# Attention on one Trainium2 core: four score banks, two product banks, and row sums from a column of ones beside the values

## The chip, the cores and the metric

The kernel runs on one core of a Trainium2 chip. The metric is the device time of one execution in microseconds; the median of repeated runs counts. The core has TensorE (PE, with PEld for its weight loads), VectorE (DVE), ScalarE (ACT), GpSimd (POOL) and SyncE (SP), each with a queue of its own that it works through in order. TensorE writes its results to PSUM, which this program divides into eight banks of 128 partitions by 512 numbers of 4 bytes.

## The reference

One step of a streaming encoder: attention, an MLP, a gated linear recurrence, and a second MLP, each with a norm before it and a sum with its input behind it. There are 1024 prompt frames and 64 frames of a running stream, 1088 in all, 1024 features, 16 query heads in 4 groups that share a key and value head of 64. Only the attention bears on the change. A chunk is 64 frames; a frame reads its own chunk and the two before it, so 192 keys. Every head has a learned sink, which enters the denominator and no value.

```python
def banded_sink_attention(q, k, v, valid, sinks):
    B, N, Q = q.shape[:3]
    qg = q.reshape(B, N, Q, N_KV, GROUP, HEAD_DIM)
    s = jnp.einsum('bnqkgd,bnskd->bnkgqs', qg, k,
                   preferred_element_type=jnp.float32) * (HEAD_DIM ** -0.5)
    s = jnp.where(valid[None, :, None, None, None, :], s, -jnp.inf)
    sink = sinks.astype(jnp.float32).reshape(N_KV, GROUP)[None, None, :, :, None, None]
    m = jnp.maximum(jnp.max(s, axis=-1, keepdims=True), sink)
    e = jnp.exp(s - m)
    p = e / (jnp.sum(e, axis=-1, keepdims=True) + jnp.exp(sink - m))
    o = jnp.einsum('bnkgqs,bnskd->bnqkgd', p.astype(v.dtype), v)
    return o.reshape(B, N, Q, N_HEADS, HEAD_DIM)
```

## The kernel before

The program runs attention (to about 356 us of the profile), the first MLP, the recurrence and the second MLP, one after the other. All products with weight matrices are done in two parts: a weight and an input are each split into a rounded half and a rest (`whi`, `wlo`, `xh`, `xl`), and each 128 x 128 block takes three matmuls (lines 93 to 95) into one bank of the pool `mm` (lines 107 and 108). VectorE takes a finished bank away. The pool `mm` has three banks for the whole program. The attention's own pool `psA` has five: two `sc`, two `pt`, one `po`. An MLP adds five banks to `mm`, the recurrence four of its own.

**Attention.** `heads(g)` goes over group g in nine steps m. Steps 0 to 7 take two chunks each (index i), step 8 the running stream. The four heads of a group stand as two tiles u = 0 and 1: the queries and keys of tile u lie in partitions 64u to 64u + 63, each tile with two heads of 64 frames, so 128 rows of scores. `scores(m)` does, for a step:

- the scores (line 306): for each i and u a matmul over 64 partitions into the bank `sc` of tile u, 192 columns (64 and 128 in step 0);
- the row maximum (311, 313), its comparison with the sink (316), and the sink's exponent (317) on VectorE;
- the exponentials on ScalarE (321), one for each i and u, from `sc` into `p`; each also sums its row into `den` (`accum_out`), which the profile shows as a second instruction, ACTIVATION_READ_ACCUMULATOR;
- the sink's exponential (324), its sum with `den` (325) and the reciprocal (326).

`values_(m)` does the rest: for each u it transposes `p` in three blocks into a bank `pt` (334), which ScalarE copies to `ptts` (335); it multiplies these with the values, `vone` and `vtok`, into `po` (340); VectorE multiplies `po` with `den` into `ob` (353); `ob` is transposed into a bank `pq` (358, the same bank as `po`), and ScalarE copies that into `pair` (363), the group's output. `vone` is built by GpSimd in each step (line 290): it holds the middle 64 keys of the two chunks, apart, so that one matmul serves both.

**What sets the order.** The step's scores are written one step ahead of its values. `mixed()` interleaves `heads(g)` with a generator of other products: the queries of group g + 1 for g = 0 to 2 (`q_group`), the output product `mix_out` for g = 3. That is only the order of writing. The framework then goes over the program with a scheduler of its own, which puts each engine's instructions in the order in which it takes them to become ready; a tile of a pool is ready when a buffer is free. So the number of buffers of a pool bears on the order of every engine. In what follows, fill means products that stand between the steps of `heads`. Behind the last step of group 3, `mix_out` takes its fourth input (`take`, which calls `split`, 162 and 163) and adds the products with `wb` (408), six matmuls each.

Of the kernel before, what the change touches and what calls it, by code (L numbers as in the profile page):

```python
# [8 lines left out]
F32 = mybir.dt.float32  # L9
# [4 lines left out]
ALU = mybir.AluOpType  # L14
AX = mybir.AxisListType
PSUM = bass.MemoryType.PSUM

P = 128
# [9 lines left out]
NKV = 4  # L28
# [7 lines left out]
class Trunk:  # L36
    def __init__(self, ctx, tc, A, O):
        self.ctx, self.tc, self.nc, self.A, self.O = ctx, tc, tc.nc, A, O
        nc = self.nc
        self.cp = ctx.enter_context(tc.tile_pool(name="const", bufs=1))  # L40
        self.wp = ctx.enter_context(tc.tile_pool(name="weights", bufs=2))
        cp = self.cp
        nc.scalar.preload_act_table_set("natural_log_exp_and_others")
        self.mm = ctx.enter_context(tc.tile_pool(name="mm", bufs=3, space=PSUM))
        self.more, self.turn = None, 0

        self.queue = nc.sync
# [51 lines left out]
    def scaled(self, c):  # L99
        if c in self.due:  # L100
            self.due.remove(c)
            self.norm_scale(c)
# [49 lines left out]
    def norm_scale(self, c):  # L152
        nc = self.nc
        s, n = self.CH[c]
        ps = self.bank()
        nc.tensor.matmul(ps[:, :n], self.ones[:], self.ss[:, s:s + n], start=True, stop=True)  # L156
        self.inv_root(self.rstd[:, s:s + n], ps[:, :n], n, D)
# [8 lines left out]
    def attention(self):  # L166
        nc, tc, A, O = self.nc, self.tc, self.A, self.O
        with ExitStack() as ctx:
# [50 lines left out]
            vone = [ap.tile([P, 2, 64], F32, name=f"vone{i}") for i in range(3)]  # L219
# [3 lines left out]
            def values(t):  # L223
                nc.sync.dma_start(O["v"][t], vt[:, t, TP - 128:T])
                for b in range(0, 9, 4):
                    pt = psA.tile([P, 4, P], F32, name="pt", tag="pt", bufs=2)
                    if b < 8:
                        for i in range(4):
                            nc.tensor.transpose(pt[:, i, :], vt[:, t, (b + i) * P:(b + i + 1) * P], self.ident[:])
                        nc.scalar.copy(vtok[:, b:b + 4, t * P:(t + 1) * P], pt[:])  # L230
                    else:
                        nc.tensor.transpose(pt[:, 0, :], vt[:, t, T - P:T], self.ident[:])
                        nc.scalar.copy(vtok[64:, 9, t * P:(t + 1) * P], pt[64:, 0, :])
# [48 lines left out]
            def heads(g, qs):  # L282
                o = self.xp[g] = self.pair(g)

                def scores(m):
                    cs = (2 * m, 2 * m + 1) if m < 8 else (16,)
                    ni = len(cs)
                    if m < 8:
                        vo, dv = vone[m % 3], slice(g * 64, g * 64 + 64)
                        nc.gpsimd.tensor_copy(vo[:64, 0, :], vtok[:64, m, dv])  # L290
                        if m:
                            nc.gpsimd.tensor_copy(vo[64:, 1, :], vtok[64:, m - 1, dv])
# [26 lines left out]
                    for u in range(2):  # L319
                        for i, (kn, off) in enumerate(sp):  # L320
                            nc.scalar.activation(pb[:, u, off:off + kn], ps[u][:, i, :kn], AF.Exp,  # L321
                                                 bias=nmax[:, u, i:i + 1], scale=0.125,
                                                 accum_out=den[:, u, i:i + 1])
                    nc.scalar.activation(es[:, :, :ni], es[:, :, :ni], AF.Exp)
                    nc.vector.tensor_add(den[:, :, :ni], den[:, :, :ni], es[:, :, :ni])
                    nc.vector.reciprocal(den[:, :, :ni], den[:, :, :ni])
                    return m, cs, ni, 2 * ni, den, pb

                def values_(m, cs, ni, nu, den, pb):
                    kts = range(0 if 0 < m < 8 else 1, 3)  # L330
                    for u in range(2):
                        pt = psA.tile([P, 4, P], F32, name="pt", tag="pt", bufs=2)
# [4 lines left out]
                    dv = slice(g * 64, g * 64 + 64)  # L337
                    for u in range(2):
# [3 lines left out]
                        if m == 0:  # L342
                            term(1, po[:, 0, u, :64], vone[0][:, 0, :], True, True)
                            term(2, po[:, 1, u, :64], vtok[:, 0, dv], True, True)
                        elif m < 8:
                            term(1, po[:, :, u, :64], vone[m % 3][:], True, False)
                            term(0, po[:, 0, u, :64], vtok[:, m - 1, dv], False, False)
                            term(2, po[:, 1, u, :64], vtok[:, m, dv], False, True)
                        else:
                            term(1, po[:, 0, u, :64], vtok[:, 9, dv], True, False)  # L350
                            term(2, po[:, 0, u, :64], vtok[:, 8, dv], False, True)
                    ob = ap.tile([P, 4, 64], F32, name="ob", tag="ob")
                    nc.vector.tensor_tensor(ob[:, :nu, :].rearrange("p (i u) d -> p i u d", u=2), po[:, :ni, :, :64],
                                            den[:, :, :ni].rearrange("p u i -> p i u").unsqueeze(3)
                                            .to_broadcast([P, ni, 2, 64]), ALU.mult)
# [559 lines left out]
```

## Time and profile before

| | us |
|---|---|
| runs without a profile, three | 2586.03, 2586.2, 2589.6 (median 2586.2) |
| profiled execution, its time | 2588.19 |
| profiled execution, its span | 2586.4 |
| mean clock granted to TensorE | 0.997 of full |
| attention, from the first instruction to the end of its fill | 0 to about 350 |

In the rows of the profile, a group reads: line, engine, operation, output<-inputs, shape, x count, then busy time in us and the mean of one in ns, then idle time of the engine just before and what ended it. A row of the timeline reads: start in us, duration in us, engine, line, operation, output<-inputs, shape, x count, and in brackets the idle time before it and the releaser. Several records of one kind in a row are joined, and the duration of a matmul goes to its modelled end, so that neighbours overlap; the distance between two starts is what an instruction cost the queue. A matmul of two fp32 operands leaves two records. In a row like "ACT p L321: 5.1, 16" under a line stand the idle us before a line's instructions, by what ended them, and how often.

### The profile page before, as it was taken

The page shows a single profiled execution, that of the slowest core. Times are in us where ns is not written, and L with a number is a line of the kernel's source. Part 1 is how long each engine was busy: PE and PEld are TensorE (multiplying, and loading weights), DVE is VectorE, ACT ScalarE, POOL GpSimd, SP SyncE. Part 2 cuts the span into 40 slices and gives each one's busy share as a digit, 9 for nine tenths or more (in the row PEclk, how much of TensorE's full clock was granted, in tenths as well). Part 3 has the DMA queues.
Part 4 walks back from the last instruction along what each step waited for, and adds up shares of the span by engine and source line. Part 5 has one row for each costly group of instructions (what it writes and reads, how often), then busy time and mean ns, then how long its engine had stood idle before and what let it go on. Part 6 is the DMA issues. An engine that isn't in the chain of part 4 may idle for free.

```text
span 2586.4 us, 40870 instructions
## 1 busy us (share of the span) xinstructions
PE 2555.1 (99%) x16788; PEld 2495.6 (96%) x16788; DVE 1324.6 (51%) x2693; ACT 913.8 (35%) x2071; POOL 61.6 (2%) x152
## 2 busy tenths in 40 slices
PE   8999999999999999999999999999999999999998
PEld 7998899999999999999999999998999999999997
DVE  7555455333333333376677777876433333333337
ACT  5336544122122122154555555635312211211223
POOL 3201100000000000000000000000000000000000
PEclk9999999999999999999999999999999999999999
DMA  5312111111111111131111111121111111111112
GB/s 167 85 46 65 37 63 41 42 49 41 49 41 46 45 41 50 42 109 49 36 36 37 37 37 37 41 93 34 50 41 50 41 45 46 41 50 41 50 41 82
DMA packets 84074, 134.07 MB, mean 52 GB/s; under 512 B 25440, under 2 KB 36320, under 8 KB 82208
## 3 DMA queue, kind: packets, MB, share of 16 engines
q1 hardware_dynamic: 79456, 119.17, 14.6%
q0 software_dynamic: 4432, 12.29, 1.6%
q8 instruction: 132, 2.16, 0.4%
q14 instruction: 54, 0.44, 0.1%
HBM read 114.39 MB, written 10.49 MB: 48 GB/s over the span
## 4 chain that ended last, share of the span: by engine, by line
PE 85%; DVE 1%; ACT 0%; issue 0%; ACTq 0%; DVEq 0%
PE mm L93 26%; PE mm L94 26%; PE mm L95 26%; PE pb L587 2%; PE pb L551 1%; PE pb L674 1%; PE pb L646 1%; PE pb L676 1%; PE pb L689 0%; PE pb L618 0%; DVE y L733 0%; PE pv L529 0%; PE pb L633 0%; PE mm L156 0%; PE pb L560 0%
## 5 line engine op out<-in xcount | busy, mean ns | idle before, releaser
L93 PE MATMUL mm<-xh,whi 128*128 128x362 f32 (+3 forms) x2944 | 978.7, 333 | 13.7 <-ACT whi L83 12.1
L94 PE MATMUL mm<-xl,whi 128*128 128x362 f32 (+3 forms) x2944 | 973.0, 331 | 0.0
L95 PE MATMUL mm<-xh,wlo 128*128 128x362 f32 (+3 forms) x2944 | 970.3, 330 | 0.0
L93 PEld LDWEIGHTS mm<-xh,whi 128*128 128x128 f32 x2944 | 554.0, 188 | 22.1 <-ACT whi L83 12.1
L94 PEld LDWEIGHTS mm<-xl,whi 128*128 128x128 f32 x2944 | 554.1, 188 | 5.5 <-issue 3.3
L95 PEld LDWEIGHTS mm<-xh,wlo 128*128 128x128 f32 x2944 | 554.5, 188 | 3.2 <-issue 0.9
L83 ACT CAST whi<-raw 128x512 fp32r<-128x512 f32 (+1 forms) x374 | 211.5, 611 | 812.2 <-PE mm L94 804.3
L93 PE MATMUL mm<-hh,whi 128*128 128x362 f32 (+1 forms) x1440 | 472.8, 328 | 0.0
L94 PE MATMUL mm<-hl,whi 128*128 128x362 f32 (+1 forms) x1440 | 472.6, 328 | 0.0
L95 PE MATMUL mm<-hh,wlo 128*128 128x362 f32 (+1 forms) x1440 | 470.6, 327 | 0.0
L727 DVE TENSOR_TENSOR pair<-pair,mm 128x362 f32<-128x362 f32 (+3 forms) x384 | 204.1, 532 | 423.4 <-PE mm L95 423.1
L95 PEld LDWEIGHTS mm<-hh,wlo 128*128 128x128 f32 x1440 | 271.4, 188 | 0.0
L93 PEld LDWEIGHTS mm<-hh,whi 128*128 128x128 f32 x1440 | 270.5, 188 | 0.0
L94 PEld LDWEIGHTS mm<-hl,whi 128*128 128x128 f32 x1440 | 270.1, 188 | 0.0
L718 DVE SCALAR_TENSOR_TENSOR r<-mm,ss 128x362 f32<-128x362 f32 (+1 forms) x192 | 102.5, 535 | 319.0 <-PE mm L95 319.0
L84 DVE TENSOR_TENSOR wlo<-raw,whi 128x512 fp32r<-128x512 f32 (+1 forms) x374 | 240.2, 678 | 4.3 <-ACT whi L83 3.6
L719 ACT ACTIVATE r<-r 128x362 f32<-128x362 f32 (+1 forms) x192 | 96.8, 505 | 353.7 <-DVE r L718 353.7
L721 DVE TENSOR_TENSOR hl<-r,hh 128x362 fp32r<-128x362 f32 (+1 forms) x192 | 102.6, 535 | 142.4 <-ACT hh L720 142.4
L720 ACT CAST hh<-r 128x362 fp32r<-128x362 f32 (+1 forms) x192 | 94.9, 495 | 5.8
L492 DVE TENSOR_TENSOR z<-mm,ss 128x384 f32<-128x384 f32 (+1 forms) x96 | 50.7, 532 | 67.1 <-PE mm L95 66.3
L408 DVE TENSOR_TENSOR pair<-pair,mm 128x384 f32<-128x384 f32 (+1 forms) x84 | 43.8, 529 | 39.1 <-PE mm L95 38.7
L321 ACT ACTIVATE p<-sc,nmax 128x192 f32<-128x192 f32 (+2 forms) x136 | 54.4, 414 | 22.9 <-DVE nmax L316 20.0
(215 smaller groups left out, 2114.4 us busy)
## 6 DMA issues: line engine op xcount, KB each, us to landing
raw<-in_w_up SPq DMA_DIRECT2D x128, 256.0 KB, 3.0
raw<-in_w_down SPq DMA_DIRECT2D x128, 256.0 KB, 2.8
raw<-in_w_in SPq DMA_DIRECT2D x64, 256.0 KB, 2.7
raw<-in_w_qkv POOLq DMA_DIRECT2D x24, 256.0 KB, 3.3
pair<-in_x SPq DMA_DIRECT2D x4, 1088.0 KB, 5.2
x_keep<-pair SPq DMA_DIRECT2D x4, 1088.0 KB, 4.7
pair<-x_keep SPq DMA_DIRECT2D x4, 1088.0 KB, 6.9
out_y<-y SPq DMA_DIRECT2D x16, 208.0 KB, 1.9
```

The lines of the kernel that those rows point to most:

```text
L83: nc.scalar.copy(hi[:, a:a + b, :], raw[:, :b, :])
L84: nc.vector.tensor_sub(lo[:, a:a + b, :], raw[:, :b, :], hi[:, a:a + b, :].bitcast(F32))
L93: nc.tensor.matmul(ps[:, :n], wh, ih[:, s:s + n], start=i == 0, stop=False)
L94: nc.tensor.matmul(ps[:, :n], wh, il[:, s:s + n], start=False, stop=False)
L95: nc.tensor.matmul(ps[:, :n], wl, ih[:, s:s + n], start=False, stop=i == last)
L321: nc.scalar.activation(pb[:, u, off:off + kn], ps[u][:, i, :kn], AF.Exp, bias=nmax[:, u, i:i + 1], scale=0.125, accum_out=den[:, u, i:i + 1])
L587: nc.tensor.matmul(psa[r:r + 64 - hh, i // 2, :].rearrange("p (s t) -> p s t", t=hh), d[:, i * 64:i * 64 + 64 - hh], dv[:, i * ns:(i + 1) ...
L718: nc.vector.scalar_tensor_tensor(y, ps, 0.0, self.rstd[:, s:s + n], ALU.max, ALU.mult)
L719: nc.scalar.activation(y, y, AF.Square)
L720: nc.scalar.copy(hh[:, s:s + n], y)
L721: nc.vector.tensor_sub(hl[:, s:s + n], y, hh[:, s:s + n].bitcast(F32))
L727: nc.vector.tensor_add(self.x(d)[:, s:s + n], self.x(d)[:, s:s + n], ps)
```

## The change

The banks are dealt out anew. `mm` keeps two banks instead of three; a new `add_banks` gives the MLPs six further ones instead of five and the recurrence one, so that these have eight, and seven with the recurrence's four, as they had. In attention there are four banks `sc`, one `pt`, one `po`. The first products and norms use `sc` and `pt`.

The row sum no longer comes from the exponentials. The values get a 65th column of ones (`vtok` and `vone` are 65 wide), so that `po` has the row sum in its column 64. The sum with the sink's exponential and the reciprocal move from `scores` to `values_`, behind `po` and before `ob`; they run once for a step as before.

```diff
-        self.mm = ctx.enter_context(tc.tile_pool(name="mm", bufs=3, space=PSUM))
-        self.more, self.turn = None, 0
+        self.mm = ctx.enter_context(tc.tile_pool(name="mm", bufs=2, space=PSUM))
+        self.more, self.turn, self.extra = None, 0, 0
...
+    def add_banks(self, ctx, name, n):
+        self.more, self.turn, self.extra = ctx.enter_context(self.tc.tile_pool(name=name, bufs=n, space=PSUM)), -1, n
+        ctx.callback(setattr, self, "extra", 0)
 
 
     def bank(self):
-        self.turn = (self.turn + 1) % 8
-        pool = self.more if self.more and self.turn < 5 else self.mm
+        self.turn = (self.turn + 1) % (2 + self.extra)
+        pool = self.more if self.turn < self.extra else self.mm
         return pool.tile([P, 512], F32, name="mm", tag="mm")
...
-                    b = psA.tile([P, 512], F32, name="v", tag=("sc", "pt")[c - 1], bufs=2) if c else None
+                    b = psA.tile([P, 512], F32, name="v", tag="sc", bufs=4) if c else None
...
-                self.scaled(c)
+                self.scaled(c, psA.tile([P, 512], F32, name="n", tag="pt", bufs=1))
...
-            vtok = ap.tile([P, 10, 256], F32, name="vtok")
-            nc.vector.memset(vtok[0:64, 9, :], 0.0)
-            nc.sync.dma_start(vtok[:, 8, :], A["cache_v"])
+            vtok = ap.tile([P, 10, NKV, 65], F32, name="vtok")
+            nc.vector.memset(vtok[:, :, :, 64:], 1.0)
+            nc.vector.memset(vtok[0:64, 9, :, :], 0.0)
+            nc.sync.dma_start(vtok[:, 8, :, :64], A["cache_v"].rearrange("p (g d) -> p g d", d=64))
...
-            vone = [ap.tile([P, 2, 64], F32, name=f"vone{i}") for i in range(3)]
+            vone = [ap.tile([P, 2, 65], F32, name=f"vone{i}") for i in range(3)]
...
-                    den = ap.tile([P, 2, 2], F32, name="den", tag="den", bufs=3)
                     es = ap.tile([P, 2, 2], F32, name="es", tag="es", bufs=3)
-                    ps = [psA.tile([P, 2, 256], F32, name="sc", tag="sc", bufs=2) for u in range(2)]
+                    ps = [psA.tile([P, 2, 256], F32, name="sc", tag="sc", bufs=4) for u in range(2)]
...
                             nc.scalar.activation(pb[:, u, off:off + kn], ps[u][:, i, :kn], AF.Exp,
-                                                 bias=nmax[:, u, i:i + 1], scale=0.125,
-                                                 accum_out=den[:, u, i:i + 1])
+                                                 bias=nmax[:, u, i:i + 1], scale=0.125)
                     nc.scalar.activation(es[:, :, :ni], es[:, :, :ni], AF.Exp)
-                    nc.vector.tensor_add(den[:, :, :ni], den[:, :, :ni], es[:, :, :ni])
-                    nc.vector.reciprocal(den[:, :, :ni], den[:, :, :ni])
-                    return m, cs, ni, 2 * ni, den, pb
-
-                def values_(m, cs, ni, nu, den, pb):
+                    return m, cs, ni, 2 * ni, es, pb
+
+                def values_(m, cs, ni, nu, es, pb):
...
-                            term(1, po[:, :, u, :64], vone[m % 3][:], True, False)
-                            term(0, po[:, 0, u, :64], vtok[:, m - 1, dv], False, False)
-                            term(2, po[:, 1, u, :64], vtok[:, m, dv], False, True)
+                            term(1, po[:, :, u, :65], vone[m % 3][:], True, False)
+                            term(0, po[:, 0, u, :65], vtok[:, m - 1, g, :], False, False)
+                            term(2, po[:, 1, u, :65], vtok[:, m, g, :], False, True)
...
+                    den = ap.tile([P, 2, 2], F32, name="den", tag="den", bufs=2)
+                    dn = den[:, :ni, :]
+                    nc.vector.tensor_tensor(dn.unsqueeze(3), po[:, :ni, :, 64:65],
+                                            es[:, :, :ni].rearrange("p u i -> p i u").unsqueeze(3), ALU.add)
+                    nc.vector.reciprocal(dn, dn)
                     ob = ap.tile([P, 4, 64], F32, name="ob", tag="ob")
                     nc.vector.tensor_tensor(ob[:, :nu, :].rearrange("p (i u) d -> p i u d", u=2), po[:, :ni, :, :64],
-                                            den[:, :, :ni].rearrange("p u i -> p i u").unsqueeze(3)
-                                            .to_broadcast([P, ni, 2, 64]), ALU.mult)
+                                            dn.unsqueeze(3).to_broadcast([P, ni, 2, 64]), ALU.mult)
...
+            self.add_banks(ctx, "mmB", 1)
...
-            self.more, self.turn = ctx.enter_context(tc.tile_pool(name=f"mm{layer}", bufs=5, space=PSUM)), -1
-            ctx.callback(setattr, self, "more", None)
+            self.add_banks(ctx, f"mm{layer}", 6)
```

**What moves in the queues.** The rows are instructions in program order on one engine: line, operation, output<-inputs, shape, x count; numbers behind a name tell tiles apart. Line numbers behind the changed part are 1 to 5 higher after.

PE before, group 1 around the scores of step 4 (tiles sc_1859 and sc_1860, which stand side by side within products of the next group):

```order
L334 MATMUL pt_1791<-ident_81,p0_456 128x128 x2
L358 MATMUL pq_1668<-ident_81,ob_1666 128x128 x2
L334 MATMUL pt_1791<-ident_81,p0_456 128x128
L334 MATMUL pt_1796<-ident_81,p0_456 128x128 x3
L306 MATMUL sc_1859<-kd1_467,qs_1069 128x192 x2
L306 MATMUL sc_1860<-kd1_467,qs_1069 128x192 x2
L93 MATMUL mm_2647<-xh5_70,whi_2332 128x384
```

PE after, the second score tile of the same step (sc_1857; the first, sc_1856, stands 35 rows earlier, with products and transposes between):

```order
L94 MATMUL mm_2743<-xl3_76,whi_2317 128x320
L335 MATMUL pt_1740<-ident_81,p1_458 128x128 x3
L340 MATMUL po_1656<-vone0_459,ptts_456 128x65
L340 MATMUL po_1656<-vtok_452,ptts_456 128x65
L340 MATMUL po_1656<-vone0_459,ptts_456 128x65
L340 MATMUL po_1656<-vtok_452,ptts_456 128x65
L310 MATMUL sc_1857<-kd1_468,qs_1064 128x192 x2
L95 MATMUL mm_2743<-xh3_68,wlo_2318 128x320
```

The two score tiles of a step have moved apart, and the scores run further ahead of the values. Of the 28 steps with two chunks and 192 keys, 13 have their score tiles as neighbours before and two after; the scores stand in 54 blocks before and 72 after.

PE before, a step without fill (group 1, scores of step 7, sc_2065 and sc_2066):

```order
L334 MATMUL pt_1997<-ident_81,p1_457 128x128 x3
L358 MATMUL pq_1895<-ident_81,ob_1893 128x128 x2
L334 MATMUL pt_2002<-ident_81,p1_457 128x128 x3
L306 MATMUL sc_2065<-kd1_467,qs_1069 128x192 x2
L306 MATMUL sc_2066<-kd1_467,qs_1069 128x192 x2
L340 MATMUL po_1961<-vone1_459,ptts_455 128x2x64
```

PE after, the same scores (sc_2062 and sc_2063):

```order
L310 MATMUL sc_2062<-kd1_468,qs_1064 128x192 x2
L335 MATMUL pt_1876<-ident_81,p1_458 128x128 x3
L363 MATMUL pq_1808<-ident_81,ob_1806 128x128 x2
L335 MATMUL pt_1946<-ident_81,p0_457 128x128 x3
L310 MATMUL sc_2063<-kd1_468,qs_1064 128x192 x2
L340 MATMUL po_1881<-vone0_459,ptts_456 128x2x65
```

Between the transposes of one step's second tile and the next step's first there stands pq alone, and both go through the one bank `pt`; steps 7 and 8 of group 1 and steps 0 to 7 of group 2 look like this after.

PE before, behind the last fill product of attention (group 3, steps 7 and 8):

```order
L358 MATMUL pq_3488<-ident_81,ob_3486 128x128 x2
L340 MATMUL po_3551<-vtok_452,ptts_455 128x64 x4
L358 MATMUL pq_3558<-ident_81,ob_3556 128x128
L93 MATMUL mm_3762<-xh6_71,whi_3736 128x320
L93 MATMUL mm_3770<-xh6_71,whi_3736 128x384
```

PE after, the same place:

```order
L335 MATMUL pt_3469<-ident_81,p1_458 128x128 x3
L363 MATMUL pq_3426<-ident_81,ob_3424 128x128 x2
L335 MATMUL pt_3541<-ident_81,p0_457 128x128 x2
L340 MATMUL po_3474<-vone1_460,ptts_456 128x2x65
L340 MATMUL po_3474<-vtok_452,ptts_456 128x65 x2
...
L335 MATMUL pt_3545<-ident_81,p0_457 128x128 x2
L363 MATMUL pq_3486<-ident_81,ob_3484 128x128 x2
L340 MATMUL po_3549<-vtok_452,ptts_456 128x65 x4
L363 MATMUL pq_3559<-ident_81,ob_3557 128x128
L93 MATMUL mm_3763<-xh6_71,whi_3737 128x320
```

The transposes of steps 7 (second tile) and 8 and the values of step 7 now follow the last fill product. Outside attention a few rows of PE change places at the starts of stages.

More of the change, by code (lines that the diff above doesn't have):

```diff
@@ L150, in inv_root, with norm_scale @@
         nc.vector.tensor_mul(out, out, y[:, :n])
-    def norm_scale(self, c):
+    def norm_scale(self, c, ps=None):
         nc = self.nc
         s, n = self.CH[c]
-        ps = self.bank()
+        ps = ps or self.bank()
         nc.tensor.matmul(ps[:, :n], self.ones[:], self.ss[:, s:s + n], start=True, stop=True)
@@ L225, in values @@
                 for b in range(0, 9, 4):
-                    pt = psA.tile([P, 4, P], F32, name="pt", tag="pt", bufs=2)
+                    pt = psA.tile([P, 4, P], F32, name="pt", tag="pt", bufs=1)
                     if b < 8:
@@ L229, in values @@
                             nc.tensor.transpose(pt[:, i, :], vt[:, t, (b + i) * P:(b + i + 1) * P], self.ident[:])
-                        nc.scalar.copy(vtok[:, b:b + 4, t * P:(t + 1) * P], pt[:])
+                        nc.scalar.copy(vtok[:, b:b + 4, 2 * t:2 * t + 2, :64], pt[:].rearrange("p b (h d) -> p b h d", d=64))
                     else:
                         nc.tensor.transpose(pt[:, 0, :], vt[:, t, T - P:T], self.ident[:])
-                        nc.scalar.copy(vtok[64:, 9, t * P:(t + 1) * P], pt[64:, 0, :])
+                        nc.scalar.copy(vtok[64:, 9, 2 * t:2 * t + 2, :64], pt[64:, 0, :].rearrange("p (h d) -> p h d", d=64))
             kd = [ap.tile([P, 1216], F32, name=f"kd{g}") for g in range(NKV)]
@@ L288, in scores @@
                     if m < 8:
[L289 to L290 removed]
+                        vo = vone[m % 3]
+                        nc.gpsimd.tensor_copy(vo[:64, 0, :], vtok[:64, m, g, :])
                         if m:
[L292 removed]
+                            nc.gpsimd.tensor_copy(vo[64:, 1, :], vtok[64:, m - 1, g, :])
                     nmax = ap.tile([P, 2, 2], F32, name="nmax", tag="nmax", bufs=3)
[L295 removed]
                     es = ap.tile([P, 2, 2], F32, name="es", tag="es", bufs=3)
[L297 removed]
+                    ps = [psA.tile([P, 2, 256], F32, name="sc", tag="sc", bufs=4) for u in range(2)]
                     sp = []
@@ L336, in values_ @@
                     po = psA.tile([P, 2, 2, 128], F32, name="po", tag="po")
-                    dv = slice(g * 64, g * 64 + 64)
                     for u in range(2):
```

14 lines of the change are left out of this document (7 added, 7 removed).

## The prediction

> **What bounds the kernel now.** I read the page first: the busy shares, then the chain that ended last.
>
> ```profile
> PE 2555.1 (99%) x16788; PEld 2495.6 (96%) x16788; DVE 1324.6 (51%) x2693; ACT 913.8 (35%) x2071; POOL 61.6 (2%) x152
> PE 85%; DVE 1%; ACT 0%; issue 0%; ACTq 0%; DVEq 0%
> ```
>
> TensorE is the bound, and ScalarE and VectorE stand in the chain with 1% between them. An edit therefore counts by what it does to TensorE's queue. Only attention changes in substance (the other stages keep eight or seven banks as before), so the second view is the busy time by stretch of attention, columns as in the header.
>
> ```profile
> core 0: us, PE busy (x) PEld busy (x) DVE busy (x) ACT busy (x) POOL busy (x), PEclk, DMA share, GB/s
> 90.00:216.00 126.00, 126.00 (x825) 115.81 (x824) 67.87 (x188) 53.78 (x210) 15.56 (x40) 1.00 0.22 57
> 216.00:245.00 29.00, 27.71 (x180) 23.27 (x178) 13.16 (x48) 19.64 (x85) 2.34 (x10) 0.94 0.31 78
> 262.00:292.00 30.00, 29.21 (x204) 25.46 (x203) 15.44 (x54) 18.71 (x80) 1.99 (x8) 1.00 0.11 38
> 330.00:356.00 26.00, 24.14 (x165) 23.46 (x164) 9.59 (x21) 9.27 (x27) 1.61 (x3) 1.00 0.09 31
> ```
>
> While a group of heads has products of the next group to fill with (90 to 216), PE is busy for all of 126 us. In the two stretches without fill it idles 1.3 and 0.8 us, and 1.9 us at the tail. So there are two regimes: with fill, only PE's own instruction time counts; without it, the round trips through ScalarE and VectorE count too. The third view is the timeline of PE around the score products (L306).
>
> ```profile
> 98.79 0.93 PE L306 MATMUL sc<-kd,qs 64*128 64x192 f32 x8
> 99.64 0.55 PE L334 MATMUL pt<-ident,p 128*128 128x128 f32 x3
> 123.40 0.91 PE L306 MATMUL sc<-kd,qs 64*128 64x192 f32 x4
> 124.24 0.42 PE L93 MATMUL mm<-xh,whi 128*128 128x320 f32 x1
> 124.49 0.31 PE L94 MATMUL mm<-xl,whi 128*128 128x320 f32 x1
> 124.64 0.31 PE L95 MATMUL mm<-xh,wlo 128*128 128x320 f32 x1
> 124.88 0.91 PE L306 MATMUL sc<-kd,qs 64*128 64x192 f32 x4
> 125.73 0.42 PE L93 MATMUL mm<-xh,whi 128*128 128x320 f32 x1
> ```
>
> This is the row on which most of the forecast rests. A step m has two score tiles; tile u uses rows 64u to 64u+63 of the array. (Each fp32 matmul leaves two records.) Where both tiles stand back to back, the eight records take 99.64 − 98.79 = **0.85 us**. Where three products stand between them, each half takes 0.84 us by itself (123.40 to 124.24, 124.88 to 125.73): **1.69 us** for the same work. Neighbours on different row halves run at the same time; the order in PE's queue decides whether they do.
>
> [...]
>
> **The change part by part.**
>
> *Lost overlap (T1).* With four score banks the scheduler no longer has to put both tiles of a step at the same moment: in the order of after, only steps 1 and 2 of group 0 still have the two tiles as neighbours. Before there were eight full ones, the first at 98.79 and the last at 289.79; two stay, six lose 0.83 us: 5.0. Other neighbours were worth less:
>
> ```profile
> 289.79 0.93 PE L306 MATMUL sc<-kd,qs 64*128 64x192 f32 x8
> 155.37 0.72 PE L306 MATMUL sc<-kd,qs 64*128 64x64 f32 x8
> 88.84 0.71 PE L306 MATMUL sc<-kd,qs 64*128 64x64 f32 x4
> 216.43 1.28 PE L306 MATMUL sc<-kd,qs 64*128 64x192 f32 x8
> 233.39 1.72 PE L306 MATMUL sc<-kd,qs 64*128 64x192 f32 x8 [0.29 <-ACT p L321]
> 267.12 0.59 PE L306 MATMUL sc<-kd,qs 64*128 64x192 f32 x4
> 325.83 0.59 PE L306 MATMUL sc<-kd,qs 64*128 64x192 f32 x2
> ```
>
> Step 0 of groups 1 to 3: two tiles in 0.65 us (0.72 less the last matmul's tail of 0.07), one alone 0.64; separated they add 0.6, 0.4 and 0.6, together 1.65. Five steps overlapped in part, between the 1.28 and the 1.72 of the rows; brought to 1.68 they add 0.9. Step 8: 267.12 has both tiles in 0.52, 325.83 one in 0.52, so +0.5, and +0.1 in group 1. Four halves are torn apart in after: two single matmuls of 0.52 instead of a pair of 0.84, 4 × 0.19 = 0.8. Sum 5.0 + 1.65 + 0.9 + 0.6 + 0.8 = **+8.9**. Bounds: +5.0 (only the six) and +10.5 (the kept two lost as well).
>
> *More switches (T2).* In after the scores stand in 72 blocks, in before in 54. By the rows above, from one product to the next is 0.15 us (124.49 to 124.64), from a product to a score 0.24 (124.64 to 124.88): 18 × 0.09 = 1.6. Returns to a product from something else fall from 93 to 85, at 0.10 each (124.24 to 124.49 is 0.25 against 0.15): −0.8. **+0.8**, between 0 and +2.4.
>
> *Waits of the scores for the exponentials go (T3).* This is what the four banks remove.
>
> ```profile
>   ACT p L321: 5.1, 16
> L306 PE MATMUL sc<-kd,qs 64*128 64x192 f32 (+2 forms) x272 | 50.6, 344 | 1.4 <-ACT p L321 1.4
> 237.47 0.91 PE L306 MATMUL sc<-kd,qs 64*128 64x192 f32 x4 [0.27 <-ACT p L321]
> ```
>
> The first row adds PE's idle time and that of its weight loads, which overlap; on PE alone it is 1.4. Measured from start to start, the six PE waits cost 0.25 to 0.36 over an unhindered step of 0.20, 1.8 together, and the loads' other ten some 0.08 each. I take **−2.6**, between −1.4 and −5.1.
>
> *One bank for transposes (T4).* The transposes of tile 1 now wait until ScalarE has copied tile 0 out of the single bank.
>
> ```profile
> L335 ACT COPY ptts<-pt 128x384 f32<-128x384 f32 x56 | 26.1, 486 | 33.5 <-PE po L340 29.9 <-PE pt L334 3.2
> 191.23 0.38 PE L358 MATMUL pq<-ident,ob 128*128 128x128 f32 x2
> 191.45 0.60 PE L334 MATMUL pt<-ident,p 128*128 128x128 f32 x4
> 232.01 0.37 ACT L335 COPY ptts<-pt 128x256 f32<-128x256 f32 x1 [0.19 <-PE po L340]
> 232.44 0.44 PE L334 MATMUL pt<-ident,p 128*128 128x128 f32 x2 [0.23 <-ACT ptts L335]
> ```
>
> With fill there are products between the two (the order shows it), and the wait costs nothing. Without fill only two transposes pq stand there: 0.22 us (191.23 to 191.45). The round trip is the last transpose's tail 0.16 (0.38 − 0.22), the copy 0.49, and two hops of 0.06 (232.01 + 0.37 = 232.38 to 232.44): 0.77, less 0.22 leaves 0.55. Behind the waiting transpose stand the next scores and the po of this step. In after ten steps have no fill (steps 7 and 8 of group 1, 0 to 7 of group 2): **+5.5**. Bounds: 0, if work queued ahead has not finished when the copy has, and all 36 steps at 0.55, +20.
>
> *The tail (T5).* The last step of group 3 has no fill behind it.
>
> ```profile
> 350.91 0.43 ACT L363 COPY pair<-pq 128x128 f32<-128x128 f32 x2 [1.92 <-PE pq L358]
> 351.40 1.10 PE L340 MATMUL po<-vtok,ptts 128*128 128x64 f32 x8 [0.52 <-ACT pair L363]
> 352.89 0.33 PE L358 MATMUL pq<-ident,ob 128*128 128x128 f32 x1 [0.39 <-DVE ob L353]
> L325 DVE TENSOR_TENSOR den<-den,es 128x4 f32<-128x4 f32 x32 | 5.1, 159 | 21.3 <-ACT es L324 10.8 <-ACT p L321 10.5
> L326 DVE RECIPROCAL den<-den 128x4 f32<-128x4 f32 x32 | 5.6, 174 | 0.7
> L353 DVE TENSOR_TENSOR ob<-po,den 128x256 f32<-128x256 f32 x32 | 13.5, 422 | 28.5 <-PE po L340 28.4
> ```
>
> Before, only pq of step 7, po and pq of step 8 come after the last product. In after the transposes of both steps and po of step 7 come there too. The first transposes of step 8 wait as in T4, 0.5. The division now starts with po: 0.16 for the sum and 0.17 for the reciprocal stand between po and ob, so pq of step 7 waits 0.16 + 0.33 + 0.42 + 0.1 of hops − 0.27 of transposes = 0.7, and pq of step 8 waits 0.4 longer. **+1.6**, between +0.7 and +4.
>
> *Two product banks (T6).* A bank is free when VectorE has added it. In the output product of the last heads a product is six matmuls, 1.04 us, so two banks leave 1.04 us of slack. Tail 0.16, a hop of 0.06, an operation as long as the add ahead of it (0.55), and the add (0.55) come to 1.3 at worst.
>
> ```profile
> 365.70 0.55 DVE L408 TENSOR_TENSOR pair<-pair,mm 128x384 f32<-128x384 f32 x1
> ```
>
> Some three such meetings at 0.3: **+0.9**, between 0 and +3. Elsewhere a product has 24 matmuls, about 4 us, and two banks do.
>
> *Ones column and sums (T7).* One column in 64 is added to these, and the accumulator reads go:
>
> ```profile
> L340 PE MATMUL po<-vtok,ptts 128*128 128x64 f32 x272 | 38.7, 265 | 0.5 <-ACT pair L363 0.5
> L340 PE MATMUL po<-vone,ptts 128*128 128x128 f32 x112 | 24.5, 301 | 0.2 <-issue 0.2
> L321 ACT ACTIVATION_READ_ACCUMULATOR p<-sc,nmax 128x1 f32 x136 | 28.1, 207 | 0.0
> ```
>
> 63.2 us / 64 is 1.0, the upper end; eight records of po at 351.40 take 1.10 and not 8 × 0.265 = 2.1, so about half of the modelled time is paid, and of that not the fixed part: **+0.3**. The sums take 28 us off ScalarE, which has 35% of the span busy; PE waits for it only as in T3 and T4, so this is 0 on the path. With fill, the longer way po, sum, reciprocal, ob, pq is covered by products; the cover gone, it is 0.33 per step, in ten steps 3.3, which I put into the range alone.
>
> Sum: 8.9 + 0.8 − 2.6 + 5.5 + 1.6 + 0.9 + 0.3 = **+15.4 us**. The profiled execution took 2588.2 us (span 2586.4 and 1.8 around it) and would become 2603.6; it lies 2.0 above the median of 2586.2, which becomes **2601.6**.
>
> **The rivals.**
>
> *Cancel.* Four banks let scores run so far ahead that the stretches without fill lose their idle time altogether (1.3 + 0.8) and the transposes' wait is hidden (T4 = 0, T3 = −5.1); T1 stays with its 5.0: 5.0 + 0.8 − 5.1 + 1.6 + 0.9 + 0.3 = +3.5, 2590. For it: ScalarE gets 28 us less to do. Against: in the order nothing but pq stands in the gap.
>
> [...]
>
> *Much slower.* The single transpose bank stalls steps with fill as well, because ScalarE's copy stands behind the next exponentials in its queue: 20 in place of 5.5, +29.9, 2616. Against: with fill several products, 0.5 us and more, stand between.
>
> *The banks don't do what is said*: scores no further ahead than before. The order of after has them further ahead, so I give this nothing of its own.
>
> **How the numbers follow.** Forecast as summed 0.66, cancel 0.19, faster 0.06, much slower 0.09. The forecast's own range is 2592 to 2609; 8 in 10 with parts of both neighbours is 2588 to 2613. A measurement of this kernel tells about 0.2%, 5.2 us, from no change: slower by more 0.76, within it 0.18, faster 0.06.
>
> **What would show it right or wrong.** T1: in the timeline of after the scores stand as x4 of 0.91, hardly an x8 of 0.93, and the sum of L306 rises from 50.6 to near 60. T3: no waits of L306 for L321. T4: waits of the transposes' rows for ScalarE's copies some 5 us, in the stretches without fill alone. T5: po of the last step to its pq some 0.4 us more than the 1.49 from 351.40 to 352.89. Beyond attention every stage lasts as long as before; a stage there that moves by over 1 us would make the working wrong, and so would separated tiles that take less than 0.84.

## The result and the profile after

| | before | after |
|---|---|---|
| median of the runs, us | 2586.51 (4 runs, 2586.03 to 2589.6) | 2610.81 (4 runs, 2610.08 to 2612.68) |
| ratio | | 1.0093, 95% interval 1.0075 to 1.0110 |
| profiled execution, us | 2588.19 | 2610.9 |
| its span, us | 2586.4 | 2609.1 |

The change makes the kernel 24.3 us slower; between the two profiled executions it is 22.7. The page of after and its busy time by stretch of attention, columns as before:

```profile
PE 2570.8 (99%) x16788; PEld 2502.3 (96%) x16788; DVE 1325.1 (51%) x2694; ACT 905.3 (35%) x1935; POOL 61.7 (2%) x152
PE 85%; DVE 1%; ACT 0%; issue 0%; ACTq 0%; DVEq 0%
90.00:216.00 126.00, 125.45 (x776) 112.94 (x776) 64.00 (x175) 44.78 (x135) 14.87 (x36) 1.00 0.22 60
216.00:245.00 29.00, 27.14 (x174) 21.43 (x174) 13.30 (x48) 16.96 (x57) 3.06 (x12) 1.00 0.19 40
245.00:262.00 17.00, 15.34 (x95) 12.06 (x96) 8.40 (x29) 10.04 (x34) 1.17 (x5) 1.00 0.19 67
```

TensorE is still the bound, with the same 16788 records, and is busy 15.7 us longer for them. In the stretch with fill it is busy as before (125.45 of 126), but gets through 776 records where it did 825. That is work that takes longer, not waiting. The groups of PE in attention say which work (busy and mean, then idle time ahead and its releaser), and the timeline shows one half of a step's scores among products:

```profile
L310 PE MATMUL sc<-kd,qs 64*128 64x192 f32 (+2 forms) x272 | 60.2, 345 | 0.0
L335 PE MATMUL pt<-ident,p 128*128 128x128 f32 x200 | 35.6, 281 | 5.6 <-ACT ptts L336 5.6
L363 PE MATMUL pq<-ident,ob 128*128 128x128 f32 x68 | 13.7, 278 | 2.3 <-DVE ob L359 2.3
...
131.14 0.91 PE L310 MATMUL sc<-kd,qs 64*128 64x192 f32 x4
131.98 0.44 PE L93 MATMUL mm<-xh,whi 128*128 128x384 f32 x1
```

The 272 records of the scores are busy 60.2 us instead of 50.6, at the same mean duration: they no longer lie over one another. From the first record of each block to the next instruction, over all blocks, it is 55.2 us in 72 blocks instead of 47.1 in 54. The wait for the exponentials is gone (0.0), and 5.6 us of waits for the copies of the single transpose bank have come. One of these waits, with ScalarE's rows:

```profile
247.61 0.44 PE L335 MATMUL pt<-ident,p 128*128 128x128 f32 x2
247.98 0.42 ACT L325 ACTIVATE p<-sc,nmax 128x192 f32<-128x192 f32 x1 [0.45 <-PE pt L335]
248.30 0.36 ACT L336 COPY ptts<-pt 128x256 f32<-128x256 f32 x1
248.71 0.55 PE L335 MATMUL pt<-ident,p 128*128 128x128 f32 x3 [0.55 <-ACT ptts L336]
```

The transposes of the first tile have ended at 248.05, but ScalarE has an exponential in front of the copy.

The timeline of PE at the tail of attention, from the transposes of step 8 to the first products of the last input (some rows between the first two are left out):

```profile
365.34 0.44 PE L335 MATMUL pt<-ident,p 128*128 128x128 f32 x2 [0.35 <-ACT ptts L336]
...
368.26 0.41 PE L363 MATMUL pq<-ident,ob 128*128 128x128 f32 x2 [0.73 <-DVE ob L359]
369.20 1.58 PE L340 MATMUL po<-vtok,ptts 128*128 128x65 f32 x8 [0.52 <-ACT pair L368]
371.65 0.45 PE L363 MATMUL pq<-ident,ob 128*128 128x128 f32 x1 [0.87 <-DVE ob L359]
372.89 0.96 PE L93 MATMUL mm<-xh,whi 128*128 128x320 f32 x2 [0.79 <-ACT xh L166]
373.64 0.52 PE L94 MATMUL mm<-xl,whi 128*128 128x384 f32 x1
373.96 0.52 PE L95 MATMUL mm<-xh,wlo 128*128 128x384 f32 x1
```

The waits are where the prediction put them: 0.35 for the copy, 0.73 and 0.87 for sum, reciprocal and `ob` (the two others, 0.52 and 0.79, were 0.52 and 0.95 in before). What it did not have is the last two rows: a product takes 0.32 us from start to start instead of 0.17. The clock granted to TensorE was halved there: it reads 0.50 from 369.75 to 376.5 by windows of a quarter of a microsecond (0.56 in the last).

Set against before at equal products, the 22.7 us lie so: 17.7 between the first score and the first product after the tail, 2.8 in the output product behind it (1.5 of them at half clock, up to 376.5), 2.25 at the start of the recurrence, 1.0 in the first 60 products, and −1.1 later, where the halved clock fell elsewhere (7.0 us from 1759.5 in before, 3.75 from 1786 in after). Before has a halved clock too in the stretch of the 17.7, from 240.5 to 244.

### The profile page after: what moved, and what is told of

The parts are those of the page before. It is cut to its first block, busy times and chain, and to the rows that moved or that the text cites. A ratio compares the mean times of both kernels' runs of the same rounds, so it can differ in the third digit from the quotient of the medians.

```text
span 2609.1 us, 40765 instructions
## 1 busy us (share of the span) xinstructions
PE 2570.8 (99%) x16788; PEld 2502.3 (96%) x16788; DVE 1325.1 (51%) x2694; ACT 905.3 (35%) x1935; POOL 61.7 (2%) x152
## 4 chain that ended last, share of the span: by engine, by line
PE 85%; DVE 1%; ACT 0%; issue 0%; ACTq 0%; DVEq 0%
PE mm L93 26%; PE mm L94 26%; PE mm L95 26%; PE pb L593 2%; PE pb L557 1%; PE pb L680 1%; PE pb L652 1%; PE pb L682 1%; PE pb L695 0%; PE pb L624 0%; PE pv L535 0%; PE pb L639 0%; PE mm L160 0%; DVE y L738 0%; DVE ss L136 0%
```

## The experiments

**Which part of the change.** The first two kernels make one half of it each. The edit of the first: the banks as after, without the column of ones (in this and the following cuts `...` marks what is left out).

```diff
-    vtok = ap.tile([P, 10, NKV, 65], F32, name="vtok")
+    vtok = ap.tile([P, 10, 256], F32, name="vtok")
...
-                         bias=nmax[:, u, i:i + 1], scale=0.125)
+                         bias=nmax[:, u, i:i + 1], scale=0.125,
+                         accum_out=den[:, u, i:i + 1])
```

> The banks as after (two for products, four for scores, one for transposes), the row sums from the exponentials as before. Theory P (the prediction's terms): the loss comes from the banks (lost overlap of score tiles, waits for the single transpose bank, two product banks), so 2600 to 2608, at least 14 of the 24 us. Rival R2 (the longer way po, sum, reciprocal, ob makes most of it): 2586 to 2595.

Measured: 2605.79 (2599.23 to 2611.38), ratio 1.0069, interval 1.0051 to 1.0087. The second keeps the banks of before and has the column of ones:

```diff
-        self.mm = ctx.enter_context(tc.tile_pool(name="mm", bufs=2, space=PSUM))
+        self.mm = ctx.enter_context(tc.tile_pool(name="mm", bufs=3, space=PSUM))
...
-    ps = [psA.tile([P, 2, 256], F32, name="sc", tag="sc", bufs=4) for u in range(2)]
+    ps = [psA.tile([P, 2, 256], F32, name="sc", tag="sc", bufs=2) for u in range(2)]
...
-    pt = psA.tile([P, 4, P], F32, name="pt", tag="pt", bufs=1)
+    pt = psA.tile([P, 4, P], F32, name="pt", tag="pt", bufs=2)
```

> The banks as before, the row sums from the column of ones as after. Theory P: +1 to +6 over before (the tail 1.6, the wider columns 0.3, and whatever the scheduler makes of it: 12 blocks with both score tiles instead of 16), 2587 to 2593. Rival R2: +12 or more, 2599 and up.

Measured: 2591.11 (2590.21 to 2592.88), ratio 1.0012 (1.0002 to 1.0022). So by the medians the banks make most of the loss, 18 us alone, and the column 3.5; R2 falls. But part of the 18 is halved clock. The four executions of the first kernel took 2599.23 at a mean granted clock of 0.998, 2605.24 and 2606.33 at 0.994, and 2611.38 at 0.991, while three of after's four had 0.997. In the one execution at 0.998 the banks alone cost 11.6. At a like clock the two halves thus add up to about 15 of the 24 us; together they cost more than apart.

**Is it the lost overlap.** Here the two score tiles of a step become one tile of two banks. All four banks stay, and so do the single transpose bank and the column, but the scheduler gets the four matmuls of a step ready at once (the part left out does the same for the first value products, which use these banks before the scores):

```diff
...
-    ps = [psA.tile([P, 2, 256], F32, name="sc", tag="sc", bufs=4) for u in range(2)]
+    pj = psA.tile([P, 2, 2, 256], F32, name="sc", tag="sc", bufs=2)
+    ps = [pj[:, u, :, :] for u in range(2)]
```

> As after, but the two score tiles of a step are one tile of two banks, in two buffers: the four banks stay, and the scheduler puts the four matmuls of a step side by side in 24 steps instead of 2. Theory P: lost overlap and switches (T1 and T2, 8 to 11 us) come back and some more, since before had 13 such steps: 11 to 20 us below after, 2591 to 2600. Rival R1 (neighbours are worth nothing on the clock, all of the loss is waits on the transpose bank and the copies): as after within 3 us, 2608 to 2614, or slower, since a step's scores now wait for both tiles' exponentials.

Measured: 2586.37 (10 runs, 2584.5 to 2586.96), 24.4 below after, and as before (ratio 0.9993, 0.9984 to 1.0003). The groups of PE in this kernel, and one step in the timeline:

```profile
L312 PE MATMUL sc<-kd,qs 64*128 64x192 f32 (+2 forms) x272 | 34.5, 347 | 0.0
L337 PE MATMUL pt<-ident,p 128*128 128x128 f32 x200 | 35.4, 281 | 3.7 <-ACT ptts L338 3.4
L365 PE MATMUL pq<-ident,ob 128*128 128x128 f32 x68 | 13.8, 279 | 5.2 <-DVE ob L361 4.9
...
116.64 0.92 PE L312 MATMUL sc<-kd,qs 64*128 64x192 f32 x8
```

Eight records in 0.92, as before at 98.79 (0.93). Over all blocks the scores take 31.7 us instead of the 55.2 of after: 23.5 of the 24.4 us. Transposes and pq together wait 8 to 9 us here as well, as in after, so waits are not what the edit removed. That the time comes out as before's doesn't mean that all of the loss was lost overlap: before's scores took 47.1, so 8.1 were lost, and the other 15.4 are pairs that before did not have. They make up for losses that stay, among them the 2.8 us in the output product and the 2.25 at the start of the recurrence, which this kernel has too. One doubt is left: the edit also moves instructions. The next two kernels take the overlap away and move less (the scores stand in 44 blocks for the joint kernel's 42, and in 69 for after's 72). Both score tiles use rows 64 to 127 of the array; first in the joint kernel, then in after.

```diff
-    r = slice(64 * u, 64 * u + 64)
+    r = slice(64, 128)
```

> The joint kernel with both score tiles on rows 64 to 127 of the array (both use the queries and keys of the second two heads, so the first two heads' scores are not the reference's). Order and waits stay nearly as they are, the overlap cannot be. Theory P (neighbours on different row halves run at the same time, and that is what the joint tile brought): 23 steps at 0.83 us, 19, less up to 6 where the longer scores cover a wait: 2599 to 2606, about the time of after less what its switches cost. Rival R1 (the joint kernel is faster because of shorter waits and fewer switches, not of overlap): 2586 to 2591.

> The kernel after with both score tiles on rows 64 to 127 (the first two heads' scores are not the reference's). Its two tiles stand apart in all but two steps. Theory P: nothing overlaps there, so no change but for those two steps, +0 to +3: 2608 to 2615. [...]

Measured: the joint kernel goes from 2586.37 to 2605.57 (2604.5 to 2613.74), after from 2610.81 to 2610.13 (2609.09 to 2624.54). The timeline of the joint kernel on one half of the rows:

```profile
118.52 1.56 PE L312 MATMUL sc<-kd,qs 64*128 64x192 f32 x8
128.57 1.56 PE L312 MATMUL sc<-kd,qs 64*128 64x192 f32 x8
```

The same eight neighbours take 1.56 us instead of 0.92, in all blocks 51.1 instead of 31.7: +19.4, against +19.2 in the whole time. Where the tiles stand apart, as in after, the rows make no difference. R1 falls: neighbours on different row halves ran at the same time (0.92 us for the eight records), separated ones did not, or after would have lost time on one half as well, and the difference was paid in full.

**The joint tile on before's banks**, one buffer of two banks instead of two of one:

```diff
...
-    ps = [psA.tile([P, 2, 256], F32, name="sc", tag="sc", bufs=2) for u in range(2)]
+    pj = psA.tile([P, 2, 2, 256], F32, name="sc", tag="sc", bufs=1)
+    ps = [pj[:, u, :, :] for u in range(2)]
```

> As before, but the two score tiles are one tile of two banks with one buffer, so that the four matmuls stand side by side in 24 steps instead of 13. Theory P: 11 to 14 further steps at 0.83 us, 9 to 12 us, less longer waits for both tiles' exponentials where there is no fill (up to 6): 2574 to 2584. Rival R1: nothing gained and the waits longer, 2588 to 2596.

Measured: 2586.51 (2581.88 to 2592.17), ratio 0.9994 (0.9985 to 1.0003): no change in the median, between the two theories. The group of the scores:

```profile
L309 PE MATMUL sc<-kd,qs 64*128 64x192 f32 (+2 forms) x272 | 36.2, 356 | 9.7 <-ACT p L324 9.7
```

The busy time falls from 50.6 to 36.2 us, over all blocks from 47.1 to 33.1, and the scores now wait 9.7 us for the exponentials, against 1.4 before: a step needs both tiles free. Gain (14.0) and wait (8.3) were both underrated, and some 6 us of gain are left. The halved clock can account for them: the profiled execution has a mean clock of 0.994, before's 0.997, which is worth up to 8 us by estimate (0.003 of 2586). The two executions of this kernel with 0.997 took 2581.88 and 2582.22, in the range of theory P.

**The column with the joint tile.** Two kernels set the joint tile and the banks of after beside the sums of before, the second with a third buffer for p:

```diff
+                         accum_out=den[:, u, i:i + 1])
...
-    pbuf = [ap.tile([P, 2, 384], F32, name=f"p{i}") for i in range(2)]
+    pbuf = [ap.tile([P, 2, 384], F32, name=f"p{i}") for i in range(3)]
...
-    pb = pbuf[m % 2]
+    pb = pbuf[m % 3]
```

> The banks of after with the joint score tile, the row sums from the exponentials as before. If the waits of the transposes pq for VectorE (7 us in the trace of the joint kernel, sum and reciprocal in their way) are paid, they shrink and the tail too: 2579 to 2584. Rival: the 28 us that return to ScalarE delay the copies as much: 2586 to 2590.

> As the joint score tile with sums from the exponentials, and a third buffer for the weights p, so that an exponential no longer waits for the transposes of two steps before and the copies behind it on ScalarE's queue come earlier. If these waits (8 us of transposes waiting for copies in the joint kernel) are paid: 3 to 5 us below the kernel with two buffers, 2575 to 2581. Rival: the buffer only lets the order change, nothing beyond 1 us.

Measured: 2604.34 (2600.01 to 2606.14) and 2601.39 (2596.97 to 2603.72). Both forecasts missed: the kernels are 15 to 18 us slower than the joint one, far over what a rival priced. The timeline of ScalarE in the first shows the accumulator reads, the windows of 30 us the clock (the column before the last two):

```profile
213.48 0.42 ACT L327 ACTIVATE p<-sc,nmax 128x192 f32<-128x192 f32 x1
213.79 0.21 ACT L327 ACTIVATION_READ_ACCUMULATOR p<-sc,nmax 128x1 f32 x1
213.88 0.43 ACT L327 ACTIVATE p<-sc,nmax 128x192 f32<-128x192 f32 x1
...
214.85 0.32 PE L312 MATMUL sc<-kd,qs 64*128 64x64 f32 x1 [1.07 <-ACT p L327]
...
210.00:240.00 30.00, 25.36 (x170) 19.28 (x169) 14.11 (x52) 18.48 (x80) 2.25 (x9) 0.91 0.29 76
240.00:270.00 30.00, 26.69 (x145) 21.54 (x143) 10.34 (x37) 14.81 (x62) 2.34 (x10) 0.73 0.00 1
```

An exponential holds ScalarE 0.40 us with its read (213.48 to 213.88). The scores then wait up to 1.07 us for it where there is no fill, and in these 60 us the granted clock falls to 0.91 and 0.73: 30 × 0.09 + 30 × 0.27 = 10.8 us at most, by estimate, that the clock costs there. The joint kernel has 1.00 in the same windows. So the column of ones, which costs some 3.5 us on before's banks, is worth about 18 where the two score tiles go together. Much of the 18 can be clock: the two profiled executions have 0.991 and 0.997 of it over their spans of 2598.2 and 2584.2, which is worth up to 16 us by estimate (0.006 of 2598), and the spans differ by 14.0. How much is clock and how much ScalarE's chain itself was not separated.

Now with the column of ones: first the joint kernel with the third buffer for p, by the same two lines, then the joint tile with one buffer on the banks of before:

> The banks and the column of after, the joint score tile in two buffers, and a third buffer for the weights p. ScalarE then no longer holds an exponential (and the copies behind it) until the transposes of two steps before have read p. If the 8 us of transposes waiting for copies come from that order on ScalarE's queue: 3 to 6 us below the joint kernel, 2580 to 2583. Rival (with one transpose bank the copy's own 0.49 is the wait, whatever stands ahead of it): 2585 to 2588.

> The banks of before, one joint score tile of two banks in one buffer, and the row sums from the column of ones. The kernel with the joint tile on before's banks gained 17 us of PE time on scores and their switches and gave 12 back in waits, 8.5 of them scores waiting for the exponentials. An exponential without its accumulator read holds ScalarE some 0.1 us less, four in a row 0.4. Theory P (the waits are ScalarE's chain, the column shortens it): 3 to 7 us below before, 2580 to 2584. Rival (the column's longer way po, sum, reciprocal, ob and the longer tail cost as much as they save, as they did on before's banks with two score tiles): 2586 to 2590.

Measured: 2585.38 (ratio 0.9992, 0.9983 to 1.0001) and 2585.11 (0.9989, 0.9980 to 0.9998). The third buffer is worth 1 us at most; its rival held. (The 8 us of its expectation are not paid as such: on PE alone the transposes of the joint kernel wait 3.4 us for copies.) The last kernel has the lowest median of all, 2.5 us below before and not clear of the third buffer's, less than was forecast:

```profile
L308 PE MATMUL sc<-kd,qs 64*128 64x192 f32 (+2 forms) x272 | 36.9, 349 | 3.4 <-ACT p L323 3.3
L338 PE MATMUL po<-vone,ptts 128*128 128x130 f32 (+1 forms) x128 | 27.9, 300 | 3.4 <-ACT pair L366 3.4
```

The wait for the exponentials falls from 9.7 to 3.3 us as said, and part of it comes back in the column's longer way, as the rival had it: the values now wait 3.4 us for ScalarE's copies of pq (0.0 without the column), and pq waits 2.0 instead of 1.0.

**The two other prices.** Two product banks in attention on the program of before, with after's dealing of banks in the other stages:

```diff
-        self.mm = ctx.enter_context(tc.tile_pool(name="mm", bufs=3, space=PSUM))
+        self.mm = ctx.enter_context(tc.tile_pool(name="mm", bufs=2, space=PSUM))
...
+            self.add_banks(ctx, "mmB", 1)
...
+            self.add_banks(ctx, f"mm{layer}", 6)
```

> As before, with only the product banks dealt as after: two in attention (one bank idle), eight and seven elsewhere. The scores stand in the same 54 blocks. The prediction's T6 gives +0.9 (0 to 3) in the output product; the trace of after shows a further 2.25 us at the start of the recurrence, in the kernels that have the new dealing and in no other. If both belong to the product banks, 2588 to 2592 and 2.25 us in that place. Rival: the recurrence's 2.25 us come from elsewhere, then 2586 to 2589.

Measured: 2589.55, ratio 1.0007 (0.9997 to 1.0016). The whole is within the noise of the halved clock, but the places can be read: +1.3 us in the output product (T6), and 2.25 us at the start of the recurrence, whose waits on PE in this kernel are

```profile
1158.31 0.41 PE L93 MATMUL mm<-xh,whi 128*128 128x384 f32 x1 [0.71 <-DVE pair L731]
1172.51 0.45 PE L93 MATMUL mm<-xh,whi 128*128 128x384 f32 x1 [0.82 <-DVE n L149]
```

The first releaser is the MLP's last sum: the recurrence now gets a product bank that the MLP is still emptying. In before these waits do not exist; after and all kernels here with its dealing of banks lose the same 2.2 to 2.3 us there.

And one transpose bank on the program of before:

```diff
...
-    pt = psA.tile([P, 4, P], F32, name="pt", tag="pt", bufs=2)
+    pt = psA.tile([P, 4, P], F32, name="pt", tag="pt", bufs=1)
```

> As before, with one transpose bank instead of two (one bank idle, two of the first value products in other banks). In the order both score tiles are neighbours in 9 steps instead of 16 blocks. Theory P: T4 with 5.5 us and five to seven lost neighbours at 0.83, 4 to 6 us: 2595 to 2600. Rival R3 (one transpose bank costs nothing by itself, since the wait is shorter than the work that can stand in it): 2590 to 2593, the lost neighbours alone.

Measured: 2598.8 (2597.3 to 2600.81), ratio 1.0043 (1.0028 to 1.0058). The sum fits theory P, its parts do not. The groups of its transposes and values:

```profile
L334 PE MATMUL pt<-ident,p 128*128 128x128 f32 x200 | 36.3, 286 | 0.9 <-ACT ptts L335 0.8
L340 PE MATMUL po<-vone,ptts 128*128 128x128 f32 (+1 forms) x128 | 27.4, 296 | 1.3 <-issue 0.7 <-ACT pair L363 0.6
```

Transposes wait 0.8 us for copies, not 5.5. The scores cost 4.2 us more (51.3 us over all blocks), and from 227.75 to 237.75 the clock was halved, for 10 us where before has 3.5, worth up to some 3 us by estimate (half of the 6.5). The rest of the 11 us is not separated. So one transpose bank alone is not cheap, but what can be read of its price lies in the scores and the clock and hardly in its own waits; those come to 5.6 us only together with the other edits. The kernel with after's banks and the old sums shows 1.9 there. What puts these waits together exactly is open.

## Why the prediction was right, and where its sizes were off

The direction, the place and the main mechanism held. The 2610.81 us lie in the range of 2588 to 2613, at its far end, but 1.8 beyond the 2609 at which the summed forecast's own range ends; the sum was 9 us too small. By the forecast's steps:

- **T1, lost overlap, +8.9**: the blocks of the scores measure +8.1. Joint tile and single row half show it both ways, by 23.5 and 19.4 us, each with the time of the whole kernel following. Taking the other row half away from after changed nothing (2610.13): across what stands between the tiles there, matmuls over all 128 rows, there was no overlap to lose.
- **T3, waits for the exponentials, −2.6**: the six waits of before cost 0.45 to 0.56 from start to start, −1.9 over the unhindered 0.20.
- **T4, single transpose bank, +5.5 by ten steps at 0.55**: 13 waits in the trace, one of them in the tail, which cost 7.7 us from start to start over the unhindered 0.11 from pq to a transpose. Duration and count were both low. The three waits with ScalarE free cost 0.51 to 0.57, the 0.55 of the forecast; in the ten others the copy stands behind an exponential, as at 248.30, and six of these cost 0.72. The ten steps were counted by the scores, but these run two to three steps ahead of the transposes in after, so that more steps of transposes fall into the stretch without fill.
- **T5, tail, +1.6**: the copy's 0.35, the 0.73 of pq, and 0.87 instead of 0.39 make 1.6. The sum is exact, partly by luck, since the wait for the copy was 0.15 shorter than forecast and the two others nearly as much longer. And the tail cost more all the same: from po to its pq it is 2.45 instead of 1.49, 0.96 more and not 0.4, half of it by the halved clock from 369.75 (the eight records of po take 1.58 instead of 1.10).
- **T6, product banks, +0.9**: 1.3 on before's program, 1.3 in after apart from the clock.
- **"Beyond attention every stage lasts as long as before"** was wrong: 2.25 us at the start of the recurrence, over the 1 us that the prediction itself named as a sign against its working. Equal counts of banks were taken for equal costs; which bank comes first, and who still holds it, was not looked up in the order.
- T2 and T7, 1.1 together: 17.7 − 8.1 − 7.7 + 1.9 − 1.2 (the two waits of pq in the tail, less the 0.39 of before) leaves 2.6 us. Two further waits of pq, 0.33 each, and the halved clock of both kernels lie in it as well; no run separated these, so whether the two terms were right is open.
- The offset: before's profiled execution lies 1.7 above the median of its four runs (2.0 above that of the three which the prediction had), after's 0.1 above its own. Taking the profiled difference for the medians' lost 1.6 us.

The chance of a faster kernel, 0.06, fell with T1, and the cancelling rival with T4, which cost 7.7 us instead of being hidden. The much slower one came nearer to the time than the sum, 2616 for 2610.8, by half of its mechanism: copies do stand behind exponentials, but in the steps without fill; steps with fill did not stall.

## What to carry to other kernels

Where matmuls used half of the array's rows, neighbours on different halves took the time of one of them (0.85 us for both tiles), and with other work between them the time of both (0.84 each); ask of every edit to buffers what it does to who stands beside whom. More buffers gave the scheduler the freedom to pull them apart, and one joint tile for what must run together took that freedom away again without giving up a bank. On the engine that is the bound, look at the clock behind a wait as well as at its length: behind the 1.26 us of idle time in the tail of after it was halved for 6.75 us, behind the 1.86 us around before's tail it stayed at 1.00; that the waits brought it down was not shown.

## What the runs showed of the hardware

In windows of a quarter of a microsecond the clock granted to TensorE read 1.00 or 0.50, but for those in which it changed. It was 0.50 in stretches of 3.5 us (before, from 240.5), 6.75 (after, from 369.75) and 10.25 (the kernel with the joint tile and the old sums, from 244.75), and in one of at least 23 (the same with the third buffer, from 238). Set against the 3.4 us ahead of them, about the length of the shortest, those in attention's later part came mostly after 1.0 to 1.8 us of idle time in PE: the tail of after and of the joint kernel after 1.26, the kernel with the joint tile and the old sums three times after 1.25. But before had one after 0.27, and none after the 1.86 us idle around its tail, in two such windows (0.52 from 348.0 to 351.4, 1.34 from there to 354.8). In the kernel with the joint tile on before's banks a window with 1.32 us idle (3.42 less the 2.10 busy) was followed by none, and the next, with 1.07, by one:

```profile
228.10:231.52 3.42, 2.10 (x19) 1.53 (x17) 1.03 (x6) 2.74 (x13) 0.47 (x2) 1.00 0.36 77
231.52:234.93 3.41, 2.34 (x19) 1.70 (x15) 1.54 (x5) 2.45 (x12) 0.00 (x0) 1.00 0.30 64
234.93:241.75 6.82, 6.78 (x30) 6.25 (x30) 3.25 (x11) 3.79 (x16) 0.23 (x1) 0.50 0.51 169
```

So PE's idle time alone does not tell when the clock falls, and what does is open: windows of 3.4 us with 0.27 to 1.8 us of idle time came before a halved clock, and windows with 1.34 and 1.32 did not. In after the clock stands at 0.83 over the 20 us around the tail:

```profile
360.00:380.00 20.00, 16.73 (x96) 15.18 (x95) 8.47 (x22) 6.80 (x19) 0.54 (x1) 0.83 0.20 69
```

This is also much of the noise here: the traces have such stretches in different places, each costing up to half its length by estimate (a product takes 0.32 us instead of 0.17 from start to start), and within a kernel the executions with the lower mean clock are the longer ones (2599.23 at 0.998 to 2611.38 at 0.991 with after's banks and the old sums).
